# Expert-choice hybrid block: unread products of the router's results placed on TensorE between the steps of the choice of experts

## Chip, core and metric

The kernel runs on one core of a Trainium2 chip. The metric is device time in microseconds (us) of one execution. Engines are named as in the profile: PE is TensorE's matmul part, PEld its weight load, DVE is VectorE, ACT is ScalarE, POOL is GpSimd, SP is SyncE, whose queue (SPq) issues most DMAs.

## What is computed

Two layers of a hybrid backbone over 512 tokens of 1024 channels (256 context tokens, 256 latent tokens). After the token mixers, the output projection and a layer norm, each layer runs an expert-choice mixture of experts. The change stands inside the choice:

```
def expert_choice_ffn(u, w_router, w_e1, w_e3, w_e2):
    cap = EC_CAPACITY * n_tok // N_EXPERTS                 # 2 * 256 // 16 = 32
    aff = jax.nn.softmax((u @ w_router).astype(jnp.float32), axis=-1)
    gate, idx = lax.top_k(jnp.swapaxes(aff, 1, 2), cap)    # 32 tokens for each of 16 experts
    xs = u[bidx, idx]
    h = jax.nn.silu(einsum('becd,edf->becf', xs, w_e1)) * einsum('becd,edf->becf', xs, w_e3)
    y = einsum('becf,efd->becd', h, w_e2) * gate[..., None]
    return jnp.zeros_like(u).at[bidx, idx].add(y)
```

Layer 0 does this for the context and for the latent tokens, each with its own choice; layer 1 for the latent tokens alone, and only they are the output.

## The kernel before, in words

The layers run one after the other (`layer`). In each, attention, retention, HGRN2 and RWKV-7 are computed first, then the branches are merged, and the last third is the expert stage: `out_proj` (output projection, layer norm and, by `logits`, the router's products), `route` (the choice), `experts` (16 experts in a loop).

**The choice, `route`.** It is one chain. Router logits lie in `lg` with tokens on the 128 partitions; the softmax over 16 experts is five steps: the maximum `mx` (profile: tile `rmx`, L1516), the difference (L196, `tt`), the exponential on ACT (L193), the sum `sm` (tile `rsm`, L1519), its reciprocal **in place** (L1520) and the product. Two TensorE transposes turn the result so that experts lie on partitions; DVE copies it to `aft` (tile `pa`, L1529). Then four rounds find the 32 largest of 256 affinities per expert, eight a round:

```
m8 = T([64, 8], "m8", bufs=2)
for i in range(CAP // 8):
    src = aft if i == 0 else wk
    nc.vector.max(m8[R], src[R])
    nc.vector.match_replace(wk[R], m8[R], src[R], -1.0)
```

`m8` is taken from its pool once, ahead of the loop: all four rounds write the same tile (profile: tile `m`, L1535 the maximum, L1536 the replacement). Then come a comparison, a running sum (L1539) and a product that give each chosen token its slot, two transposes back (`w<-ident,pa`), a copy to `pt` (L1546), and the first `gather`: one-hot matrices `oh` from `pt`, and products `h<-oh,x` that collect the tokens of the first four experts into `xg`. `R` is rows 0 to 63 in layer 0 and 32 to 63 in layer 1.

**The experts.** Each of the 16 has three 1024x1024 fp32 weights, 12 units of 1 MB, which SP's queue fetches in order into a ring of rooms (`ring`, `mid`, `low`, `late`, in layer 1 also `pair`; `expert_weights`, L1600 and L1604). A unit's DMA is issued when its room's last reader has finished. The ring is filled ahead while `route` runs; after that a fetch waits for the products of an expert.

**PSUM.** In the expert stage three tags share it: `h` (3 banks), `y` (2), `w` (3). `self.mm` (L211) is one matmul; an fp32 matmul shows as two records in the trace. The order of each engine's queue is that of the program. A tile that is overwritten waits for its readers, on whatever engine they are.

Of the kernel before, what the change touches and what calls it, by code (L numbers as in the profile page):

```python
# [18 lines left out]
P = 128  # L19
# [157 lines left out]
class Block:  # L177
# [1321 lines left out]
    def route(self, l, lo, x, sc, sh, lg, xg, pool, xpool):  # L1499


        nc = self.nc
        t0, s0 = lo // 128, lo // 256
        r0 = 32 * s0
        ns = 2 - s0
        pa = pool.tile([64, 2, 256], F32, tag="pa", name="pa")
        pos, aft = pa[:, 0], pa[:, 1]
        T = lambda shape, tag, dt=F32, bufs=1: pool.tile(shape, dt, tag=tag, name=tag, bufs=bufs)
        lv = lg[:, t0:, :].rearrange("p (s j) e -> p s j e", j=2)
        tmp = xpool.tile([P, 1024], F32, tag="oht", name="tmp")  # L1510
        af = tmp[:, 0:128].rearrange("p (j s e) -> p j s e", j=2, s=2)
        mx, sm = T([P, ns, 2], "rmx"), T([P, ns, 2], "rsm")
        nc.gpsimd.memset(af, 0.0)

        av = af.rearrange("p j s e -> p s j e")[:, s0:, :, 0:E]
        nc.vector.tensor_reduce(mx, lv, AX.X, ALU.max)  # L1516
        self.tt(av, lv, mx.unsqueeze(3).to_broadcast([P, ns, 2, E]), ALU.subtract)
        self.act(av, av, AF.Exp)
        nc.vector.tensor_reduce(sm, av, AX.X, ALU.add)  # L1519
        nc.vector.reciprocal(sm, sm)  # L1520
        self.tt(av, av, sm.unsqueeze(3).to_broadcast([P, ns, 2, E]), ALU.mult)
        ps = self.psum("w")
        for j in range(2):
            self.tr(ps[0:64, 128 * j:128 * j + 128], af[:, j].rearrange("p s e -> p (s e)"))
        R = slice(r0, 64)
        if s0:
            nc.gpsimd.memset(aft[0:32], 0.0)
            nc.gpsimd.memset(pos[0:32], -1.0)
        nc.vector.tensor_copy(aft[R], ps[R, 0:256])  # L1529

        wk, mk, ones = [tmp[0:64, 256 * i:256 * i + 256] for i in (1, 2, 3)]
        m8 = T([64, 8], "m8", bufs=2)
        for i in range(CAP // 8):
            src = aft if i == 0 else wk
            nc.vector.max(m8[R], src[R])  # L1535
            nc.vector.match_replace(wk[R], m8[R], src[R], -1.0)  # L1536
        self.ts(mk[R], wk[R], 0.0, ALU.is_lt)
        nc.gpsimd.memset(ones, 1.0)
        nc.vector.tensor_tensor_scan(pos[R], ones[R], mk[R], 0.0, ALU.mult, ALU.add)  # L1539
        self.tt(pos[R], pos[R], mk[R], ALU.mult)  # L1540

        ps = self.psum("w")
        for j in range(2):
            self.tr(ps[:, 64 * j:64 * j + 64], pos[:, 128 * j:128 * j + 128])
        pt = T([P, 2, 2, 32], "pt")
        nc.vector.tensor_copy(pt.rearrange("p j s e -> p (j s e)"), ps[:, 0:128])  # L1546

        def gather(e0, dst, tag):

            n = dst.shape[2]  # L1550
            w = 32 * n
            whole = w < 256
            if not whole:
                room = xpool.tile([P, 2, 4, 256], F32R, tag="hl", name="xhl", bufs=1)
            for s in range(s0, 2):
                if not whole or s == s0:
                    ohs = xpool.tile([P, 1 + whole, 2, n, 32], F32 if whole else F32R, tag="oht", name="oh", bufs=1)
                oh = ohs[:, whole and s]
                for j in range(2):
                    self.tt(oh[:, j], pt[:, j, s, e0:e0 + n].unsqueeze(2).to_broadcast([P, n, 32]),  # L1560
                            self.iota.unsqueeze(1).to_broadcast([P, n, 32]), ALU.is_equal)
                for k in range(KT):
                    xk = x[:, 2 * s - t0:2 * s - t0 + 2, 128 * k:128 * k + 128]
                    xs = [xk]
                    if not whole:
                        xs = [room[:, i, k % 4].rearrange("p (t c) -> p t c", c=128) for i in range(2)]
                        self.split(*xs, xk)
                    ps = self.psum(tag)[:, 0:w]
                    for j in range(2):
                        for v in xs:  # L1570
                            self.mm(ps, v[:, j], oh[:, j].rearrange("p e c -> p (e c)"), start=(j == 0 and v is xs[0]),
                                    stop=(j == 1 and v is xs[-1]))
                    d = dst[:, k, :, 32 * (s - s0):32 * (s - s0) + 32]
                    src = ps.rearrange("p (e c) -> p e c", c=32)
                    if k % 2:
                        self.act(d, src, AF.Identity, bias=sh[:, k, s:s + 1], scale=sc[:, k, s:s + 1])
                    else:
                        self.ts(d, src, sc[:, k, s:s + 1], ALU.mult, sh[:, k, s:s + 1], ALU.add)

        gather(0, xg, "h")  # L1580
        return pa, gather
# [472 lines left out]
```

## Time and profile before

| | |
|---|---|
| time of 3 runs, median | 2281.23 us (2278.9 to 2287.31) |
| the profiled execution's own time | 2285.33 us |
| its span, first to last instruction | 2283.5 us |
| mean granted TensorE clock | 0.930 |
| busy: PE, DVE, ACT, POOL | 88%, 46%, 28%, 12% |
| DMA, mean over the span | 243 GB/s, 554.90 MB |

The span lies 1.8 us under the execution's own time. A granted clock of 1.00 is TensorE's higher level, 2.4 GHz, and 0.50 the lower, 1.2 GHz. Times in the rows are microseconds from the start of the span. Layer 0's choice lies at 792 to 812, layer 1's at 1826 to 1841.

### The profile page before, as it was taken

Reading aid. Unit: us, or ns where it says so; the run is one execution under the profiler, and the core shown is the slowest. Engines: PE = TensorE matmul, PEld = TensorE weight load, DVE = VectorE, ACT = ScalarE, POOL = GpSimd, SP = SyncE. Lnnn points to the kernel's source line nnn. Section 1 sums busy time; section 2 is a strip of 40 time slices with the busy share of each in tenths; the row PEclk is TensorE's granted clock in tenths of the full one; section 3 lists DMA queues with packets and bytes.
Section 4 is the critical chain, followed back from the end, with each engine's and each line's share of the span. In section 5 each row is a group of like instructions: output and inputs, shape, how many; then the busy total and the mean of one; then the engine's idle time right before and its main releaser. Section 6 shows DMA issues by size and latency. Waiting matters only on the chain. (4 is left out here: it accounts for less than half of the span.)

```text
span 2283.5 us, 38233 instructions
## 1 busy us (share of the span) xinstructions
PE 2004.9 (88%) x16294; PEld 1263.6 (55%) x16294; DVE 1039.2 (46%) x2174; ACT 630.4 (28%) x1044; POOL 270.8 (12%) x188
## 2 busy tenths in 40 slices
PE   6998999999999899999998898999899887676675
PEld 3657747777687744333332656777788753222222
DVE  3548755855523526222222666758764642020112
ACT  3453445413323212000000454464343320000000
POOL 2000201222242000000000200103353000000000
PEclk8999999999999999999999899998999889777777
DMA  8264242111252587999999555224223899999996
GB/s 321 84 218 149 80 129 79 36 48 60 103 191 88 230 350 304 426 425 425 426 426 424 203 171 191 67 76 151 87 92 130 319 389 423 425 424 424 424 424 280
DMA packets 96939, 554.90 MB, mean 243 GB/s; under 512 B 11296, under 2 KB 13280, under 8 KB 46848
## 3 DMA queue, kind: packets, MB, share of 16 engines
q1 hardware_dynamic: 95312, 543.93, 61.1%
q0 software_dynamic: 912, 6.42, 0.7%
q8 instruction: 128, 2.10, 0.4%
q10 hardware_dynamic: 544, 2.10, 0.3%
q14 instruction: 43, 0.35, 0.0%
HBM read 549.13 MB, written 3.28 MB: 242 GB/s over the span
## 5 line engine op out<-in xcount | busy, mean ns | idle before, releaser
L221 POOL TENSOR_TENSOR wl<-wr,wh 128x1280 fp32r<-128x1280 f32 (+1 forms) x62 | 179.1, 2888 | 317.0 <-ACT wh L193 314.0
L211 PE MATMUL m<-mh,wh 128*128 128x512 f32 (+1 forms) x512 | 190.0, 371 | 6.0 <-ACT th L193 5.0
L193 ACT ACTIVATE wh<-wr 128x1024 fp32r<-128x1024 f32 (+1 forms) x126 | 143.3, 1138 | 157.4 <-PE pj L211 69.4
L211 PE MATMUL m<-mh,wl 128*128 128x512 f32 (+1 forms) x512 | 177.6, 347 | 2.5 <-POOL wl L221 1.9
L211 PE MATMUL m<-ml,wh 128*128 128x512 f32 (+1 forms) x512 | 177.3, 346 | 0.0
L211 PE MATMUL h<-late,later 128*32 128x256 f32 (+1 forms) x880 | 139.5, 538 | 30.0 <-DMA late<-in_w_e_dram 29.8
L206 DVE SCALAR_TENSOR_TENSOR h<-h 128x512 f32<-128x512 f32 (+1 forms) x32 | 17.7, 554 | 299.8 <-ACT h L193 299.8
L221 DVE TENSOR_TENSOR wl<-wr,wh 128x1024 fp32r<-128x1024 f32 (+1 forms) x64 | 78.9, 1235 | 103.9 <-ACT wh L193 103.3
L193 ACT ACTIVATE h<-h 128x512 f32<-128x512 f32 (+1 forms) x32 | 15.7, 491 | 396.9 <-PE h L211 396.9
L211 PEld LDWEIGHTS m<-mh,wh 128*128 128x128 f32 x512 | 100.8, 197 | 32.4 <-issue 14.4
L196 DVE TENSOR_TENSOR h<-h 128x512 f32<-128x512 f32 (+1 forms) x32 | 17.7, 554 | 214.5 <-PE h L211 214.5
L211 PE MATMUL h<-ring,later 128*32 128x256 f32 (+1 forms) x640 | 94.0, 543 | 19.7 <-DMA ring<-in_w_e_dram 19.7
L211 PEld LDWEIGHTS m<-mh,wl 128*128 128x128 f32 x512 | 100.8, 197 | 13.2 <-POOL wl L221 2.1
L211 PEld LDWEIGHTS m<-ml,wh 128*128 128x128 f32 x512 | 101.1, 198 | 10.8 <-issue 2.3
L211 PEld LDWEIGHTS h<-late,later 128*32 128x32 f32 (+1 forms) x880 | 44.2, 134 | 113.3 <-issue 58.4
L193 ACT ACTIVATE ht<-w 128x512 f32<-128x512 f32 (+1 forms) x32 | 15.7, 491 | 281.7 <-PE w L216 281.7
L211 PE MATMUL y<-late,ht 128*32 128x256 f32 (+1 forms) x536 | 71.9, 494 | 8.4 <-DMA late<-in_w_e_dram 5.8
L211 PE MATMUL h<-mid,later 128*64 128x512 f32 (+1 forms) x352 | 64.2, 555 | 12.5 <-DMA mid<-in_w_e_dram 12.5
L211 PEld LDWEIGHTS h<-ring,later 128*32 128x32 f32 (+1 forms) x640 | 30.4, 137 | 73.3 <-issue 36.3
L211 PE MATMUL y<-ring,ht 128*32 128x256 f32 (+1 forms) x448 | 58.8, 492 | 13.1 <-DMA ring<-in_w_e_dram 9.7
L193 ACT ACTIVATE th<-m 128x512 f32<-128x512 f32 (+1 forms) x50 | 24.7, 493 | 164.8 <-PE m L211 164.5
L206 DVE SCALAR_TENSOR_TENSOR ht<-y,gt,g 128x512 f32<-128x512 f32 (+1 forms) x32 | 18.7, 614 | 95.9 <-PE y L211 95.7
(636 smaller groups left out, 4508.2 us busy)
## 6 DMA issues: line engine op xcount, KB each, us to landing
late<-in_w_e_dram SPq DMA_DIRECT2D x144, 1024.0 KB, 19.5
ring<-in_w_e_dram SPq DMA_DIRECT2D x109, 1024.0 KB, 19.7
mid<-in_w_e_dram SPq DMA_DIRECT2D x63, 1024.0 KB, 19.7
pair<-in_w_e_dram SPq DMA_DIRECT2D x36, 1024.0 KB, 19.6
wr<-in_wmg_dram SPq DMA_DIRECT2D x48, 640.0 KB, 4.0
mw<-in_wmod_dram SPq DMA_DIRECT2D x48, 512.0 KB, 5.8
y<-in_wmod_dram SPq DMA_DIRECT2D x48, 512.0 KB, 4.3
low<-in_w_e_dram SPq DMA_DIRECT2D x20, 1024.0 KB, 19.8
```

Of the source, the lines that this page charges most:

```text
L193: self.nc.scalar.activation(out=out, in_=in_, func=func, **kw)
L196: self.nc.vector.tensor_tensor(out, a, b, op)
L206: self.nc.vector.scalar_tensor_tensor(out, a, s, b, op0, op1)
L211: self.nc.tensor.matmul(out, lhsT, rhs, start=start, stop=stop)
L221: (eng or self.nc.vector).tensor_tensor(lo, src, hi.bitcast(F32), ALU.subtract)
```

## The change

A helper `warm(v)` in `route` issues three matmuls of 256 columns each. Their weights (the stationary operand) are a result of the chain, `v`; what streams through are rows of `x`, the block of normalised tokens. The sums go to a PSUM tile of tag `y` that nothing reads. It is called after `mx`, after `sm`, and in each of the four rounds after the maximum: six times a layer, 18 matmuls, in both layers.

```
+        def warm(v):
+            ps = self.psum("y")
+            v = v.rearrange("p a b -> p (a b)") if len(v.shape) == 3 else v
+            R = slice(r0, 64) if v.shape[0] < P else slice(0, P)
+            for i in range(3):
+                self.mm(ps[0:v.shape[1], 0:256], v, x[R, 0, 256 * (i % 2):256 * (i % 2) + 256])
...
         nc.vector.tensor_reduce(mx, lv, AX.X, ALU.max)
+        warm(mx)
         self.tt(av, lv, mx.unsqueeze(3).to_broadcast([P, ns, 2, E]), ALU.subtract)
         self.act(av, av, AF.Exp)
         nc.vector.tensor_reduce(sm, av, AX.X, ALU.add)
+        warm(sm)
         nc.vector.reciprocal(sm, sm)
...
             nc.vector.max(m8[R], src[R])
+            warm(m8[R])
             nc.vector.match_replace(wk[R], m8[R], src[R], -1.0)
```

On PE, in layer 0's `route` (layer 1's is the same with 2 columns of `rmx` and `rsm`); `wrt,u` are the router's products, `tmp` the softmax, `m` the eight maxima, `pa` the slots:

```order
 L211 MATMUL h<-wrt,u 128x16 x3
+L211 MATMUL y<-x_5595,rmx 4x256 [waits DVE_49]
+L211 MATMUL y<-x_5595,rmx 4x256 x2
+L211 MATMUL y<-x_5595,rsm 4x256 [waits DVE_49]
+L211 MATMUL y<-x_5595,rsm 4x256 x2
 L216 MATMUL w<-ident,tmp 64x128 [waits DVE_49,Pool_49]
 L216 MATMUL w<-ident,tmp 64x128
-L216 MATMUL w<-ident,pa 128x64 [waits DVE_49,PE_49]
+L211 MATMUL y<-x_5595,m_6885 8x256 [waits DVE_49,PE_49]
+L211 MATMUL y<-x_5595,m_6885 8x256 x2
+L211 MATMUL y<-x_5595,m_6885 8x256 [waits DVE_49]
+L211 MATMUL y<-x_5595,m_6885 8x256 x2
```

Six matmuls stand ahead of the first pair of transposes, and twelve (two of the four rounds are shown) between that pair and the next.

On DVE, at the same place, from the sum of the softmax to the second round:

```order
-L1520 RECIPROCAL rsm<-rsm 128x4 [waits DVE_49]
+L1529 TENSOR_REDUCE rsm<-tmp 128x4 [waits Activation_49]
+L1531 RECIPROCAL rsm<-rsm 128x4 [waits DVE_49,PE_49]
 L196 TENSOR_TENSOR tmp<-tmp,rsm 128x2x2x16 [waits DVE_49]
...
+L1546 MAX m_6885<-pa 64x8 [waits DVE_49]
+L1548 MATCH_REPLACE tmp<-m_6885,pa 64x256 [waits DVE_49]
+L1546 MAX m_6885<-tmp 64x8 [waits DVE_49,PE_49]
+L1548 MATCH_REPLACE tmp<-m_6885,tmp 64x256 [waits DVE_49]
```

No DVE instruction is added or moved, but four of them now also wait for PE in each layer: the reciprocal, which overwrites the weights `rsm`, and the maxima of rounds two, three and four, which overwrite the weights `m`. The queues of ACT, POOL and SP stand as before.

## Rows read from the trace of the kernel before

**Rows 1.** The page's 40 slices of the span, granted TensorE clock in tenths:
```profile
PEclk8999999999999999999999899998999889777777
```
**Rows 2.** Windows over layer 0's choice: busy of engines, granted clock, DMA share, GB/s:
```profile
core 0: us, PE busy (x) PEld busy (x) DVE busy (x) ACT busy (x) POOL busy (x), PEclk, DMA share, GB/s
790.00:792.00 2.00, 1.28 (x8) 1.28 (x8) 1.57 (x6) 1.17 (x2) 0.00 (x0) 0.81 0.97 406
792.00:794.00 2.00, 0.16 (x1) 0.05 (x1) 1.31 (x7) 1.46 (x4) 0.46 (x2) 0.50 1.05 442
794.00:800.00 6.00, 0.60 (x2) 0.18 (x2) 4.80 (x16) 0.00 (x0) 0.00 (x0) 0.50 1.00 421
808.00:812.00 4.00, 4.00 (x37) 4.00 (x36) 1.64 (x4) 1.87 (x5) 0.00 (x0) 0.96 0.13 53
```
**Rows 3.** Windows over layer 1's choice, same columns:
```profile
1826.00:1828.00 2.00, 0.11 (x1) 0.00 (x0) 1.20 (x7) 1.52 (x4) 0.48 (x2) 0.50 0.99 418
1838.00:1842.00 4.00, 4.00 (x41) 3.62 (x44) 1.84 (x5) 1.83 (x4) 0.00 (x0) 0.86 0.53 223
```
**Rows 4.** Timeline of DVE in layer 0's choice: start, us, engine, line, operation:
```profile
792.47 0.22 DVE L1516 TENSOR_REDUCE rmx<-lg 128x4 f32<-128x64 f32 x1
793.76 0.18 DVE L1520 RECIPROCAL rsm<-rsm 128x4 f32<-128x4 f32 x1
795.44 0.42 DVE L1535 MAX8 m<-pa 64x8 f32<-64x256 f32 x1
796.40 0.42 DVE L1535 MAX8 m<-tmp 64x8 f32<-64x256 f32 x1
798.34 0.42 DVE L1535 MAX8 m<-tmp 64x8 f32<-64x256 f32 x1
800.41 0.42 DVE L196 TENSOR_TENSOR pa<-pa,tmp 64x256 f32<-64x256 f32 x1
```
**Rows 5.** Timeline of PE, PEld and first readers in layer 0's choice and gather:
```profile
794.31 0.18 PEld L216 LDWEIGHTS w<-ident,tmp 128*64 128x64 f32 x2 [2.26 <-issue]
800.94 0.28 PEld L216 LDWEIGHTS w<-ident,pa 64*128 64x128 f32 x2 [6.45 <-issue]
802.12 10.35 PE L211 MATMUL h<-oh,x 128*128 128x128 f32 x64 [0.71 <-DVE oh L196]
803.38 0.41 DVE L202 TENSOR_SCALAR xg<-h,ra,rb 128x128 f32<-128x128 f32 x1 [0.71 <-PE h L211]
806.79 0.41 DVE L202 TENSOR_SCALAR xg<-h,ra,rb 128x128 f32<-128x128 f32 x1 [1.30 <-PE h L211]
```
**Rows 6.** Timeline of layer 1's gather, first expert products and their reader:
```profile
1836.08 5.28 PE L211 MATMUL h<-oh,x 128*128 128x128 f32 x32 [0.71 <-DVE oh L196]
1841.29 3.66 PE L211 MATMUL h<-pair,xg 128*32 128x256 f32 x64
1844.76 2.77 PE L211 MATMUL h<-ring,xg 128*32 128x256 f32 x48
1845.01 0.39 ACT L193 ACTIVATE h<-h 128x256 f32<-128x256 f32 x1 [3.16 <-PE h L211]
```
**Rows 7.** SP's queue after layer 0's choice, and layer 1's issue (timeline):
```profile
794.11 22.31 SPq L1604 DMA_DIRECT2D ring<-in_w_e_dram  x3
1843.28 2.55 SPq L1604 DMA_DIRECT2D pair<-in_w_e_dram  x4
```
**Rows 8.** Windows of both expert stages, columns as in rows 2:
```profile
808.50:814.40 5.90, 5.90 (x46) 4.55 (x46) 3.06 (x7) 2.29 (x5) 0.00 (x0) 1.00 0.01 4
812.00:910.00 98.00, 97.23 (x479) 41.89 (x479) 41.02 (x83) 15.93 (x34) 0.00 (x0) 1.00 0.83 326
910.00:1240.00 330.00, 310.41 (x1400) 105.97 (x1397) 82.73 (x156) 22.50 (x37) 0.12 (x1) 1.00 1.01 425
1844.00:2266.00 422.00, 302.06 (x3328) 127.06 (x3324) 62.05 (x152) 24.98 (x60) 0.00 (x0) 0.80 1.00 419
1999.50:2009.80 10.30, 7.86 (x72) 2.61 (x68) 0.42 (x1) 0.39 (x1) 0.00 (x0) 0.50 1.02 422
```

## The prediction

> **What bounds the kernel now.** I read the page first, then windows over the two choices of experts, then the timeline of each choice, last what follows it. The page's clock slices [rows 1] stand at 9 or 10 tenths nearly everywhere, and low in the last quarter; nothing there shows the choice, which is some 20 us of 2283. The windows do [rows 2, 3]: from 792 to 800 and from 1826 on the granted clock is 0.50, the lower of TensorE's levels (1.2 GHz), and PE is nearly idle while DVE runs the chain. In layer 0 the clock had fallen just before, inside 790 to 792 (mean 0.81), so the stretch begins cold whatever is put into it. The gather after the chain then starts cold. By the mean of 0.96 in 808 to 812 layer 0's clock rose at 808.3 (4 us x 0.04 / 0.5 = 0.3 us cold), 6.2 us after the gather began at 802.12 [rows 2, 5]; layer 1's rose at 1839.1 (0.86, so 1.1 us cold), 3.0 us after 1836.08 [rows 3, 6].
>
> The choice is on the path that sets the end, in both layers. In layer 1 the first fetch that waits for expert 0's products is issued at 1843.28, and from 1844 to 2266 the DMA share is 1.00 [rows 7, 8]: whatever delays that issue delays the end by as much. In layer 0 the queue's three `ring` fetches begin at 794.11 and take 22.31 us to be issued, since they wait for rooms, and from 808.5 to 814.4 the DMA engines move 4 GB/s [rows 7, 8]: the fetches made ahead have landed, so none covers a later gather. Then PE is busy 97.2 of 98 us up to 910 at clock 1.00, and after that DMA runs at 1.01 [rows 8]. Both start from the gather's end. So I count each microsecond of the chain once, in either layer, and half a percent (11.4 us, about what a measurement of this kernel can tell from no change) is a lot of chain.
>
> **Prices.** A new batch is three fp32 matmuls of 256 columns, six records. No row before has weights of 4 or 8 columns, so I go by columns streamed. Cold, sixteen records of 128 columns lie between the readers at 803.38 and 806.79: 0.213 us each, so 0.426 for 256 columns and **2.56 us a batch** [rows 5]. At the upper level (2.4 GHz) 64 records of 256 columns, four side by side, start over 3.47 us, 0.217 a step, so **1.30 us a batch** [rows 6]. Those are the two ends; that narrow weights make it cheaper I exclude, since a record's length follows what streams, and all six use the same columns and can't stand side by side. A PE instruction follows its DVE source by 0.11 us (`pa` ends at 800.83, its load starts at 800.94) [rows 4, 5]. A reader follows the end of the stream by 0.41 us cold (802.12 + 4 x 0.213 = 802.97, reader at 803.38) and by 0.25 warm (1844.76 to 1845.01) [rows 5, 6].
>
> **The change part by part.** It removes nothing. It adds six batches a layer, and waits of DVE for PE that the order shows at four places.
>
> *The reciprocal* overwrites `rsm`, the second batch's weights, so it waits for that batch, which queues behind the first. `rmx` ends at 792.69, the reciprocal now starts at 793.76, 1.07 later [rows 4]. Cold: 0.11 + 2 x 2.56 + 0.41 = 5.64, so 4.6 us later. If the clock rises 3.0 us into the batches, as in layer 1's gather, 7 records go cold and 5 warm: 0.11 + 3.0 + 1.08 + 0.25 = 4.44, 3.4 later. If it rises after 6.2 us, as in layer 0's gather, that is too late to help. I take the middle, **+4.0**. Behind the reciprocal on DVE stands only the chain itself; ACT and POOL have nothing else to do there, and SP waits for rooms.
>
> *The rounds.* `m8` is one tile, so the next maximum waits until the last matmul of the batch before is done. A round is 0.96 us now (795.44 to 796.40) [rows 4]. With the batch in it: 0.42 (the maximum) + 0.11 + 2.56 + 0.41 = 3.50 cold, +2.54; or 0.42 + 0.11 + 1.30 + 0.25 = 2.08 warm, +1.12. The replacement, 0.48, hides beside the batch. Three maxima wait: **+7.6** cold, +3.4 warm. Which? Between the softmax batches and the first round lie two transposes, a copy and a maximum, some 2 us with PE nearly idle, and in such an idle stretch the clock fell in both layers. Once cold, a round keeps PE at work for 2.56 of 3.50 us, 73%; the nearest row is 1999.5 to 2009.8, busy 7.86 of 10.3 us, 76%, and the clock stayed at 0.50 through it [rows 8]. So I take cold.
>
> A gap of its own between groups of matmuls is what the Trainium skill ("TensorE: Matmul & The Clock Gate", section "A second HAM failure mode: psum-queue depth-cycling") describes: it says that frequent short idling between groups makes the clock swing between its levels. By it the rounds would cost the mean, 3 x 1.83 = 5.5 instead of 7.6, and the sum below would be 18.4 instead of 22.6; the row just named speaks for the lower level.
>
> *The fourth batch* has no maximum behind it, but the transposes of `pa` stand behind it on PE. They start 2.18 us after the fourth maximum ends (798.76 to 800.94) [rows 4, 5]; the batch needs 0.11 + 2.56 = 2.67: **+0.5** cold, nothing warm, where DVE's comparison, scan and product cover it.
>
> *The gather* is what could gain. All warm it would be 64 x 0.108 = 6.9 us instead of 10.35 in layer 0, and 32 x 0.108 = 3.5 instead of 5.28 in layer 1 [rows 5, 6]: 5.2 us in all, the most there is to win. With cold rounds it starts cold again, after PE has been at work, so I take layer 1's 3.0 us before the rise for both: layer 0 saves 3.2 us of half rate, **-1.6**, layer 1 nothing.
>
> PSUM, ACT, POOL and SP cost nothing: the `y` banks are not read until expert 0's third product.
>
> **Sum.** 4.0 + 7.6 + 0.5 = 12.1 a layer, 24.2 for both, less 1.6: **+22.6 us**. The profiled execution took 2285.3 us, so 2307.9 on its own terms; it stands 4.1 above the median of the three runs, so 2303.8 against the median, 1.0% slower.
>
> **Rivals.**
>
> *The clock holds.* It rises in the softmax batches (+3.4), stays up in the rounds (+3.4, where a warm round keeps PE at work 1.30 of 2.08 us) and through the gather (-5.2 in all): 2 x 6.8 - 5.2 = +8.4, 2289.6. For it: the gathers show that products do raise the clock. Against: the 2 us of idle PE in between. The Trainium skill, same page, section "Why this matters for your kernels", advises to leave no idle gap between bursts so that the clock stays up; that is the rule for this rival, and the trace agrees with its first half: with PE idle the clock stood at 0.50 [rows 2, 3]. Even so the waits cost more than the gather returns.
>
> *One layer holds, the other not.* 6.8 - 3.4 + 12.1 in one case, 10.5 + 6.8 - 1.8 in the other: +15.5 both, 2296.7.
>
> *Products with 4 or 8 columns of weights don't raise the clock at all.* No row has such weights alone. Then 4.6 + 7.6 + 0.5 = 12.7 a layer, and layer 1's gather may run cold to its end (32 x 0.213 = 6.8, +1.5): +26.9, 2308.1.
>
> *The other side: the wait ends with the weight load.* If DVE were let go once the last of a batch's weights are in the array, the rounds would keep their 0.96 us and PE would run behind. At the upper level throughout, the first transposes would start 0.11 + 2.60 = 2.71 us after `rmx` instead of 1.62, +1.1, and four batches (5.2 us) would end 0.2 us late for `pa`: +1.3 a layer, -5.2 by the gathers, so -2.6, 2278.6. It decides where a release comes under 0.5 us after the maximum, as the replacement takes that long. Against it: an array that still streams uses its weights, and the order names PE as a whole. That the delay vanishes behind fetches (no change, the change then not doing anything) is of the same size; the DMA gap [rows 8] speaks against it.
>
> **How the numbers follow.** Forecast (cold rounds, 22.6) 0.54; nothing raises the clock 0.15; one layer holds 0.13; the clock holds in both 0.11; the other side and no effect 0.07. Slower by over 0.5%: the first three, and 0.02 of the fourth, where runs scatter: 0.84. Within: 0.09 + 0.05 = 0.14. Faster: 0.02. The range runs from the clock holding in both, 2290, to nothing raising it, 2308, and a microsecond for scatter: 2290 to 2309.
>
> **What would show it.** Right: the reciprocal 4 to 5.7 us after `rmx`, maxima 3.5 us apart, clock 0.50 over most of the rounds, the gather starting 12 us later in each choice than `rmx` now implies, DMA idle longer before the first fetch of the expert stage, and the stretch after it as long as before. Wrong: maxima 1 us apart (no wait), or 2.1 us apart at clock 1.00 with gathers of 7 and 3.5 us (the clock holds), or a delay that the later stretches don't pass on.

## The result and the profile after

The changed kernel takes **2301.32 us** (median of 6 runs, 2298.22 to 2306.87), the kernel before 2280.07 (6 runs, 2278.33 to 2287.31): a ratio of **1.0084, interval 1.0067 to 1.0101**, so 19.2 us more (15.3 to 23.0). The forecast was 22.6 more, 2303.8.

DVE's timeline over layer 0's choice (against [rows 4]) shows where the time went (layer 0, then layer 1):

```profile
787.78 0.22 DVE L1525 TENSOR_REDUCE rmx<-lg 128x4 f32<-128x64 f32 x1
792.31 0.18 DVE L1531 RECIPROCAL rsm<-rsm 128x4 f32<-128x4 f32 x1 [3.21 <-PE y L211]
793.76 0.42 DVE L1546 MAX8 m<-pa 64x8 f32<-64x256 f32 x1
795.81 0.42 DVE L1546 MAX8 m<-tmp 64x8 f32<-64x256 f32 x1 [1.12 <-PE y L211]
797.78 0.42 DVE L1546 MAX8 m<-tmp 64x8 f32<-64x256 f32 x1 [1.04 <-PE y L211]
801.02 0.42 DVE L1546 MAX8 m<-tmp 64x8 f32<-64x256 f32 x1 [2.30 <-PE y L211]
...
1833.09 0.19 DVE L1525 TENSOR_REDUCE rmx<-lg 128x2 f32<-128x32 f32 x1
1838.65 0.17 DVE L1531 RECIPROCAL rsm<-rsm 128x2 f32<-128x2 f32 x1 [4.30 <-PE y L211]
1840.06 0.42 DVE L1546 MAX8 m<-pa 32x8 f32<-32x256 f32 x1
1842.11 0.42 DVE L1546 MAX8 m<-tmp 32x8 f32<-32x256 f32 x1 [1.12 <-PE y L211]
1845.34 0.42 DVE L1546 MAX8 m<-tmp 32x8 f32<-32x256 f32 x1 [2.31 <-PE y L211]
1848.58 0.42 DVE L1546 MAX8 m<-tmp 32x8 f32<-32x256 f32 x1 [2.31 <-PE y L211]
```

The four waits stand where the order said, each released by PE's `y<-x` products. The reciprocal starts 4.31 us after `rmx` ends (788.00), before 1.07. The maxima are 2.05, 1.97 and 3.24 us apart, before 0.96; in layer 1 they are 2.05, 3.23 and 3.24. The sizes 2.0 and 3.2 are the two levels of the clock, as PE's timeline shows (against [rows 5, 6]):

```profile
788.05 2.72 PE L211 MATMUL y<-x,rmx 128*4 128x256 f32 x6 [0.90 <-DVE rmx L1525]
790.57 1.70 PE L211 MATMUL y<-x,rsm 128*4 128x256 f32 x6
796.29 1.46 PE L211 MATMUL y<-x,m 64*8 64x256 f32 x6 [0.51 <-DVE m L1546]
798.26 2.72 PE L211 MATMUL y<-x,m 64*8 64x256 f32 x6 [0.51 <-DVE m L1546]
804.15 0.48 PE L216 MATMUL w<-ident,pa 64*128 64x64 f32 x2
805.33 10.35 PE L211 MATMUL h<-oh,x 128*128 128x128 f32 x64 [0.71 <-DVE oh L196]
815.62 2.80 PE L211 MATMUL h<-ring,xg 128*64 128x512 f32 x12
...
1852.89 5.31 PE L211 MATMUL h<-oh,x 128*128 128x128 f32 x32 [0.71 <-DVE oh L196]
1858.13 3.66 PE L211 MATMUL h<-pair,xg 128*32 128x256 f32 x64
```

A batch takes 2.72 us in the records at the lower level and 1.46 at the upper. The gathers are what they were: 10.35 and 5.31 us. The windows (columns as in [rows 2]) give the clock:

```profile
788.00:790.00 2.00, 1.95 (x5) 0.60 (x6) 0.45 (x2) 0.85 (x2) 0.00 (x0) 0.50 0.98 414
790.00:792.00 2.00, 2.00 (x8) 0.64 (x6) 0.00 (x0) 0.00 (x0) 0.00 (x0) 0.74 1.04 438
796.00:798.00 2.00, 1.46 (x6) 0.44 (x6) 0.93 (x4) 0.00 (x0) 0.00 (x0) 0.97 1.03 434
798.00:800.00 2.00, 1.74 (x5) 0.57 (x6) 0.68 (x3) 0.00 (x0) 0.00 (x0) 0.50 0.99 418
804.00:806.00 2.00, 1.29 (x6) 0.96 (x6) 1.19 (x5) 0.00 (x0) 0.00 (x0) 0.50 0.01 4
810.00:812.00 2.00, 2.00 (x13) 2.00 (x13) 0.70 (x2) 0.46 (x1) 0.00 (x0) 0.62 0.00 0
```

The softmax batches do raise it: 0.74 over 790 to 792 puts the rise at 791.0, 3.0 us after the first product. It then holds over the idle stretch and two rounds, falls at 797.9, and rises again only inside the gather. In layer 1 it rises at 1838.9, 0.3 us after the softmax batches have ended, and falls after one round. The DMA share is 0.01 from 804 on: the fetches made ahead have landed, as in [rows 8], and the delay goes through to SP's queue (against [rows 7]):

```profile
1860.12 2.60 SPq L1616 DMA_DIRECT2D pair<-in_w_e_dram  x4
```

Call "the choice" the time from the end of `rmx` to expert 0's first product. It took 27.62 and 24.85 us here, 19.71 and 14.61 in the profile of before (792.69 to 812.40 and, by [rows 6], 1826.68 to 1841.29): 18.1 us more of the 19.2. Expert 0's first product in layer 0 before:

```profile
812.40 3.65 PE L211 MATMUL h<-ring,xg 128*64 128x512 f32 x16
```

What follows the second choice lasts as long as ever (442.17 us, before 442.21).

### The profile page after: what moved, and what is told of

Read it like the earlier page. It is cut to its first block, busy times and chain, and to the rows that moved or that the text cites. A ratio compares the mean times of both kernels' runs of the same rounds, so it can differ in the third digit from the quotient of the medians.

```text
span 2300.3 us, 38385 instructions
## 1 busy us (share of the span) xinstructions
PE 2029.4 (88%) x16366; PEld 1268.8 (55%) x16366; DVE 1037.0 (45%) x2174; ACT 629.9 (27%) x1044; POOL 271.3 (12%) x188
## 6 DMA issues: line engine op xcount, KB each, us to landing
mid<-in_w_e_dram SPq DMA_DIRECT2D x63, 1024.0 KB, 19.7
low<-in_w_e_dram SPq DMA_DIRECT2D x20, 1024.0 KB, 19.8
```

## Experiments

Diffs are against the changed kernel unless said otherwise.

**The parts alone.** `e2_softmax_only` keeps the two softmax batches, `e3_rounds_only` the four in the rounds, `e4_one_product` all six, each of one product:

```
 e2:  -            warm(m8[R])
 e3:  -        warm(mx)      -        warm(sm)
 e4:  -            for i in range(3):      +            for i in range(1):
```

> The batches in the four rounds are left out, the two in the softmax stay. Theory: the reciprocal starts 4.4 to 5.1 us after rmx ends, instead of 1.1, the maxima stand 0.96 us apart, the clock falls again before the gather, which takes its 10.4 and 5.3 us or up to 2 us more or less: +3.3 and +4.0, together about +7 us (5 to 10). Rival, the loss sits in the rounds alone: 0 to +2 us.

> The two batches in the softmax are left out, those in the four rounds stay. Theory: the softmax is as before, the first round starts at the lower clock and nothing in the rounds raises it, as TensorE works 2.6 of 3.4 us: maxima 3.2 to 3.5 us apart in all three waits of both layers, transposes of pa 0.5 us late, +7.4 to +8.1 a layer, together about +15.5 us (13 to 17). If instead the batches raise the clock by themselves, maxima of 2.0 us appear in the later rounds and the sum lies near +9.

> One product in a batch instead of three. Theory (the price goes by the columns streamed, in the wait of DVE): reciprocal 2.2 us after rmx ends (+1.1), maxima 1.7 to 1.8 us apart (+0.8 each, three times), pa's transposes not late: +3.6 a layer, about +7 us in both (5 to 9). Rival, the price is that of a wait between the engines and not of the products: maxima as far apart as in the changed kernel (2.0 to 3.2 us) and +12 us or more. Rival, TensorE's queue alone: the transposes half a microsecond late, +1 us in all.

Measured: ratios of 1.005 (1.0028 to 1.0072), 1.0066 (1.0043 to 1.0089) and 1.0035 (1.0019 to 1.0052). In e2 the reciprocal starts 4.54 and 5.37 us after `rmx`, the maxima are 0.97 apart and the choices 22.31 and 20.03 us. In e3 every round is cold, 3.24 us, and the choices are 27.01 and 22.25. Its window shows the clock through such rounds:

```profile
790.00:796.00 6.00, 4.53 (x12) 1.11 (x12) 2.21 (x7) 0.00 (x0) 0.00 (x0) 0.50 1.01 422
```

What follows: each part costs by itself, and both by the same wait. PE is busy 4.53 of 6 us in e3's rounds and its clock stays at 0.50. In the changed kernel the first rounds were warm because the softmax batches had raised it. In e4 rounds of 1.53 to 1.62 us show that a wait remains even for two records. Against the mean of two profiles of before (the table below) the choices cost 8.3, 15.3 and 6.0 us, each inside its expected range; the time of e2, 11.4 us more, lies above its range of 5 to 10, with an interval of 6.4 to 16.4.

**The wait taken away.** `e1_own_tiles` gives each batch weights that nobody overwrites, so DVE never waits:

```
-        nc.vector.reciprocal(sm, sm)
+        rs = T([P, ns, 2], "smr")
+        nc.vector.reciprocal(rs, sm)
...
         for i in range(CAP // 8):
+            m8 = T([64, 8], f"m8{i}")
```

> Each round writes maxima of its own tile, and the reciprocal writes a tile of its own, so no DVE step waits for a batch; the 36 products stay where they are. Theory (DVE waits for the batches whose weights it would overwrite): the reciprocal starts 1.1 us after rmx ends, the maxima stand 0.96 us apart in both layers, the transposes still queue behind the two softmax batches (about +3 us a layer), the four later batches run on without gaps beside DVE (0 to +5 us) and the gathers start at the upper clock (-3.4 and -1.8 us). Sum over both layers about +2 us on the kernel before (0 to +8), so some 15 us less than the changed kernel. Rival, TensorE's own queue delays the chain: as the changed kernel, +15 to +21. Rival, the streams slow DVE's steps by contention: the maximum takes clearly over 0.42 us and most of the loss stays.

Measured: 1.0078 (1.0055 to 1.0102), nearly the whole loss. The waits are gone (reciprocal +1.11, maxima 0.96 to 0.97 apart), but the choices still take 26.61 and 21.49 us. PE's timeline and windows of layer 0:

```profile
798.41 8.41 PE L211 MATMUL y<-x,m 64*8 64x256 f32 x24 [1.06 <-DVE m L1547]
806.75 0.47 PE L216 MATMUL w<-ident,pa 64*128 64x64 f32 x2
...
798.00:800.00 2.00, 1.59 (x8) 0.71 (x9) 1.86 (x7) 0.00 (x0) 0.00 (x0) 1.00 1.00 422
800.00:801.00 1.00, 1.00 (x5) 0.31 (x4) 0.93 (x4) 0.00 (x0) 0.00 (x0) 0.74 1.02 426
801.00:807.00 6.00, 6.00 (x16) 1.80 (x14) 2.04 (x6) 0.00 (x0) 0.00 (x0) 0.50 1.01 423
810.00:814.00 4.00, 4.00 (x21) 4.00 (x20) 0.82 (x2) 1.37 (x3) 0.00 (x0) 0.50 0.00 0
```

PE's own queue took the place of the wait: the transposes of `pa` stand behind 24 records that run 8.41 us, and start 5.58 us after the last maximum instead of 2.21. The surprise is the clock. It fell at 800.5 with PE busy without a gap, and stayed at 0.50 for six more microseconds of unbroken products. So the theory had the waits right and its sum (about 2 us) wrong: the gathers, which it had at the upper level, began cold, and the batches held up the transposes of `pa` by 3.3 to 3.4 us in each layer. The time is that of the rival in which TensorE's own queue delays the chain; but part of it lies outside the choices, as the table below shows.

**How many rows the products use.** The batches of the rounds take 64 of the 128 rows of TensorE in layer 0 and 32 in layer 1; the softmax batches take all. `e6_128_rows` makes the rounds' products 128 rows high, the added rows of weights zero, and keeps the waits; `e5_own_128` does the same with the tiles of e1:

```
 e6:  +        m8 = T([P, 8], "m8", bufs=2)
      +        nc.gpsimd.memset(m8, 0.0)
      -            warm(m8[R])
      +            warm(m8)
```

> The changed kernel with weights of all 128 rows in the rounds, one tile as before, so the maxima still wait. New theory: the clock stays at 1.00 through the rounds, maxima 2.0 us apart in all three waits of both layers, the gathers at about 7 and 3.5 us: +3 in layer 0 and +5.5 in layer 1, about +8.5 us (6 to 12), which is the rival of the prediction in which the clock holds. Rival (rows don't matter): as the changed kernel, rounds of 3.2 us and +18.

> Own tiles as in the first experiment, and in the four rounds the weights span all 128 rows (8 maxima on their rows, zeros on the others), so each batch streams 128 rows of x instead of 64 or 32; columns, places and count are the same. New theory (products over 64 or 32 rows neither raise nor hold the clock, those over 128 rows do): clock 1.00 from the end of the softmax batches on, the four batches take 1.30 us each and end about with pa (2.2 to 2.6 us after the last maximum instead of 5.5), the gathers take about 7 and 3.5 us: +0 to +2.5 a layer by the softmax batches alone, +2.5 us in all (0 to +8), against the +13.8 that the two choices took longer with own tiles alone. Rival (narrow weights don't hold the clock, whatever their rows): clock 0.50 under the batches, as with own tiles alone, +13 or more.

Measured: e6 1.0041 (1.0025 to 1.0057), e5 1.003 (1.0013 to 1.0047). DVE's maxima of e6 in layer 0, then e5's PE timeline and windows there:

```profile
795.58 0.42 DVE L1547 MAX8 m<-pa 64x8 f32<-64x256 f32 x1
797.64 0.42 DVE L1547 MAX8 m<-tmp 64x8 f32<-64x256 f32 x1 [1.13 <-PE y L211]
799.61 0.42 DVE L1547 MAX8 m<-tmp 64x8 f32<-64x256 f32 x1 [1.04 <-PE y L211]
801.59 0.42 DVE L1547 MAX8 m<-tmp 64x8 f32<-64x256 f32 x1 [1.04 <-PE y L211]
```

```profile
792.64 5.34 PE L211 MATMUL y<-x,m 128*8 128x256 f32 x24 [1.05 <-DVE m L1550]
798.96 7.41 PE L211 MATMUL h<-oh,x 128*128 128x128 f32 x64 [0.71 <-DVE oh L196]
...
792.00:794.00 2.00, 1.36 (x7) 0.63 (x8) 1.84 (x7) 0.00 (x0) 0.00 (x0) 1.00 0.99 418
794.00:798.00 4.00, 4.00 (x20) 1.56 (x19) 3.18 (x9) 0.00 (x0) 0.00 (x0) 1.00 1.02 426
798.00:800.00 2.00, 1.29 (x11) 1.15 (x12) 1.48 (x6) 0.00 (x0) 0.00 (x0) 1.00 1.03 430
```

The same 24 records take 5.34 us instead of 8.41, with no fall of the clock, and the gather is warm from its first product: 7.41 us instead of 10.35 (layer 1: 3.81 to expert 0's first product, where the changed kernel has 5.24). All four choices of e5 and e6 hold 1.00 from the rounds to the gather's end. e6's choices are 23.24 and 19.31 us, e5's 19.92 and 16.00.

**Fills without a chain.** Would products that wait for nothing gain? `g1_fill` drops `warm` and puts two products at the output projection's last tile, five before the first transposes, twelve after them, all over 128 rows; `g2_fill64` has the twelve over 64 rows (`fill(n, v)` issues n products of 256 columns with the weights `v`; nothing reads them):

```
+            if t == 3:
+                ps = self.psum("h")
+                for i in range(2):
+                    self.mm(ps[0:8, 0:256], self.ident[:, 0:8], x[:, 256 * i:256 * i + 256])
...
+        fill(5, self.ident[:, 0:8])
...
+        fill(12, tmp[:, 0:8])
```

> No weights that a step overwrites: products of 256 columns over 128 rows, with constant weights between the router's last products and ahead of the first transposes, and twelve with the softmax's result as weights between the two pairs of transposes; none has a DVE step behind it. Theory: the clock stays at 1.00 from the output projection to the gather, the chain is as long as before (at most 0.5 us longer), the gathers take about 7 and 3.5 us: 5 us less than before (-2 to -6), 0.2%. If the clock falls in the softmax all the same: twelve products at the lower clock take 10 us where there are 6, and +4 to +8.

> As the fill before, but the twelve products between the transposes run over 64 rows instead of 128 (weights and x). Nothing else differs. Theory (rows count): the clock falls within the twelve products, they end after pa is ready (0 to 3 us late), and the gathers start cold again, 9 to 10.4 and 5 to 6 us: 0 to +6 us against before, and 4 us or more over the fill with 128 rows. Rival: the same as the fill with 128 rows.

Measured: 1.0011 (0.9995 to 1.0027) and 1.0006 (0.999 to 1.0022), neither told from no change; the 5 us that g1 was to gain did not come. In g1's layer 0 the clock is 1.00 throughout and the choice takes 16.31 us, 3.4 less than before. In layer 1 it takes 15.26, as windows of g1 there show:

```profile
1826.00:1828.00 2.00, 1.20 (x6) 0.32 (x4) 1.76 (x8) 0.00 (x0) 0.00 (x0) 1.00 1.01 426
1828.00:1830.00 2.00, 0.31 (x2) 0.20 (x2) 1.44 (x4) 0.00 (x0) 0.00 (x0) 0.99 1.01 426
1830.00:1832.00 2.00, 1.67 (x8) 1.70 (x9) 0.79 (x3) 0.00 (x0) 0.00 (x0) 0.50 1.03 434
```

The products ran ahead of the chain (six records of the twelve products, written behind the first transposes, ran before them), held up those transposes by 0.9 us (2.55 after `rmx`), and ended at 1827.2; PE was nearly idle from there on, and at 1830.0 the clock fell, just ahead of the gather. g2's twelve were to lose the clock while they ran, and did not, in either layer: it stayed at 1.00 through 5.3 us of them in layer 0 and fell in the gather, at 806.2; in layer 1 it stayed at 1.00 through 5.8 us of them (with the first transposes in between) and fell at 1840.4, in the idle stretch behind them (choices 17.95 and 16.44 us). So its theory failed: products over 64 rows don't bring a fall every time. In g2 PE had been at work over 128 rows ahead of the twelve, with the clock at 1.00; in e1 and its repeat the clock had been up for only 1.0 to 2.5 us when the batches of the rounds began. No run tells whether that is the difference.

`g3_hold` combines the two: g1's first fills (but three before layer 1's transposes), and in the rounds 3, 3, 3 and 2 products over 128 rows with weights in four tiles of their own:

```
+        ms = [T([P, 8], f"m8{i}") for i in range(CAP // 8)]
...
+            src, m8 = aft if i == 0 else wk, ms[i]
...
+            fill(3 - (i == 3), m8)
```

> Products that hold the clock without a wait of DVE: fills over all 128 rows, with the identity's columns as weights where no result of the chain is needed (two at the output projection's last tile, five in layer 0 and three in layer 1 ahead of the first transposes), and in the rounds three, three, three and two products whose weights are four tiles of their own, 128 rows high, so that each batch starts after its maximum and no maximum waits. Theory (row count and the gaps of PE set the clock; waits of DVE and the queue of PE set the loss): maxima 0.96 us apart, reciprocal 1.1 us after rmx, first transposes at most 0.3 us late, those of pa at most 0.3 late, granted clock 1.00 from the output projection to the end of both gathers, gathers 7.3 and 3.8 us instead of 10.3 and 5.2; the choices together 3 to 5 us shorter than before, the time 0.1 to 0.2% under before. Rival (the fills cost on PE what the gathers return, as in the fill kernel's layer 1): choices within 1 us of before, ratio 1.000. Second rival (the clock falls in the gaps between the small batches): 0.50 within the rounds, gathers of 9 us and more in layer 0, and the choices longer than before.

Measured: 1.0012 (0.9998 to 1.0027), no gain. Layer 0 went as the theory has it (choice 16.18 us, gather 7.34). In layer 1 the clock fell at 1829.4 (0.85 over 1828 to 1830), in the idle stretch before the rounds. The 22 records took 7.79 us, so that the transposes of `pa` started 4.89 us after the last maximum instead of 2.21. But these products, over 128 rows, raised the clock again at 1836.2, 5.9 us after the first of them, and the gather was warm (3.81 us); the choice took 15.26. Together the choices are still 2.9 under the first profile of before, and the time does not show it.

**What scatters.** Three kernels were profiled a second time.

> The kernel before once more, for a second profile of the stretches outside the choices. Theory (what the kernels differ by outside their choices is scatter of single executions): the choices last 19.7 and 14.6 us again within 0.3, while the start of layer 0's choice, the stretch between the choices and the one after the second differ from the first profile by 2 to 6 us. Rival (these stretches are fixed and the changed kernels lengthen them): they repeat within 1 us.

> The changed kernel once more. Theory (the clock's rise and fall in the choice are set by what PE did before, not by chance): reciprocal 4.3 and 5.4 us after rmx, maxima 2.0, 2.0, 3.2 us apart in layer 0 and 2.0, 3.2, 3.2 in layer 1, gathers 10.3 and 5.2 us, choices 27.6 and 24.9 us long, all within 0.3. Rival (the moment of the fall scatters): the number of rounds that run at the upper level differs from the first profile, by 1.2 us of choice for each; the choices then lie between 23 us and 29 us.

> The kernel with a weight tile of its own for every batch once more, since the moments of the clock's rise and fall turned out to scatter from one execution to the next. Theory (products over 64 or 32 rows don't raise the clock): after the fall, granted clock 0.50 to the end of the batches although PE is busy without a break for more than 4 us, in both layers; last maximum to the transposes of pa 4.5 to 5.9 us; gathers over 8.8 and over 4.9 us; the choices at least 24 and 20 us long. Rival (the first profile's low clock was chance): in at least one layer the clock rises within the batches, those transposes come 2.5 us after the last maximum as with 128 rows, and that gather takes 7.3 or 3.8 us.

`s1_before_again`: `rmx` of layer 0 ends at 804.32, before 792.69, so what precedes the choice scatters by 11.6 us. The choices take 18.34 and 15.33 us (before 19.71 and 14.61). They did not repeat within 0.3: the clock's rise in the gather moved, by 1.4 us of choice in layer 0 and 0.7 the other way in layer 1, while the sum moved by 0.7. `s2_after_again`: 29.69 and 25.46 us, so the rival was right that the number of warm rounds is not fixed, though 29.69 lies above its 29. Its maxima in layer 0:

```profile
796.56 0.42 DVE L1546 MAX8 m<-pa 64x8 f32<-64x256 f32 x1
798.94 0.42 DVE L1546 MAX8 m<-tmp 64x8 f32<-64x256 f32 x1 [1.45 <-PE y L211]
802.18 0.42 DVE L1546 MAX8 m<-tmp 64x8 f32<-64x256 f32 x1 [2.30 <-PE y L211]
805.41 0.42 DVE L1546 MAX8 m<-tmp 64x8 f32<-64x256 f32 x1 [2.31 <-PE y L211]
```

Only part of the first round is warm here. `s3_own_again`, which is e1 once more: 25.12 and 18.70 us. In layer 0 as in e1; in layer 1 the clock held over 4.4 us of products over 32 rows and then fell, again with PE busy:

```profile
1836.70:1839.00 2.30, 2.27 (x11) 0.96 (x12) 2.16 (x7) 0.00 (x0) 0.00 (x0) 1.00 1.01 427
1839.00:1841.00 2.00, 2.00 (x11) 0.77 (x9) 1.79 (x6) 0.00 (x0) 0.00 (x0) 1.00 1.01 422
1841.00:1842.00 1.00, 1.00 (x4) 0.35 (x3) 0.50 (x2) 0.00 (x0) 0.00 (x0) 0.55 0.98 410
1842.00:1843.00 1.00, 1.00 (x5) 0.19 (x2) 0.00 (x0) 0.00 (x0) 0.00 (x0) 0.50 1.06 442
```

There the theory's lower bounds (4.5 us to the transposes, choices of 24 and 20) were missed: 3.34 us, and 18.70 in layer 1. What repeats in all four choices with own tiles over 64 or 32 rows is the fall under unbroken work, and a cold start of the gather (8.96 to 10.28 us, 5.18 to 5.63).

**A loss that is not in the choice.** Set side by side, over both layers and against the mean of the two profiles of before (34.0 us), the time against its median of 2280 us:

| kernel | choices, us more | time, us more (interval) | fetch rate, GB/s, 960 to 1240 us |
|---|---|---|---|
| changed (2 profiles) | +19.8 | +19.2 (15.3 to 23.0) | 426 |
| e1 (2 profiles) | +12.0 | +17.8 (12.5 to 23.3) | 421 |
| e2 | +8.3 | +11.4 (6.4 to 16.4) | 425 |
| e3 | +15.3 | +15.0 (9.8 to 20.3) | 426 |
| e4 | +6.0 | +8.0 (4.3 to 11.9) | 426 |
| e5 | +1.9 | +6.8 (3.0 to 10.7) | 421 |
| e6 | +8.6 | +9.3 (5.7 to 13.0) | 425 |
| g1 | -2.4 | +2.5 (-1.1 to 6.2) | 425 |
| g2 | +0.4 | +1.4 (-2.3 to 5.0) | 425 |
| g3 | -2.6 | +2.7 (-0.5 to 6.2) | 421 |

The kernels with four tiles of their own lose 5 to 6 us more than their choices do. All four profiles of them fetch the experts' weights at 421 GB/s, all ten others at 425 or 426. The page's rate slices and the row of its issues, the changed kernel's and then e1's:

```profile
GB/s 319 89 213 146 92 115 78 48 47 60 165 133 135 231 299 311 426 425 425 426 425 408 172 185 184 69 113 116 81 98 152 325 313 424 425 424 423 424 424 282
late<-in_w_e_dram SPq DMA_DIRECT2D x144, 1024.0 KB, 19.5
```

```profile
GB/s 319 95 211 142 83 124 78 48 47 48 146 157 121 237 299 306 422 421 421 421 421 420 197 175 194 57 110 120 86 96 146 327 337 420 421 421 421 421 421 289
late<-in_w_e_dram SPq DMA_DIRECT2D x144, 1024.0 KB, 19.8
```

The bytes are the same; a unit lands 0.3 us later. 1.0% of the 330 us of layer 0 that DMA bounds [rows 8] is 3.3 us, and the stretch after the second choice is 443.8 to 444.5 us in those four profiles, 440.8 to 442.2 in the others: 2.6 more. Sum 5.9. (g1's difference is as large at 425, within its interval of 3.7 either way: it is the rate that shows the loss, not the differences.) In the built programs the small tiles move one kind of room, `late`, which takes 144 of the 384 units: its rooms start at a multiple of 256 bytes of a partition in before, the changed kernel, e2, e3, e4, e6, g1 and g2, 96 bytes behind one in e1 and e5, 64 in g3. All other rooms stay, 64 or 128 bytes off. The Trainium skill ("DMA: Bandwidth & Descriptors", section "How a descriptor splits into AXI transactions") says that a descriptor which does not start at a multiple of 256 bytes spends beats on bytes that it fetches and throws away. It does not say whether that holds for the side that is written, and only that side moved here. By its way of counting, a row of 8 KB that starts 96 bytes off takes 259 beats instead of 256, which over 144 of 384 units is an estimate of 0.4%, less than half of what the rates show. No run moved the rooms alone, so the cause is argued and not shown.

## Why the prediction was right

The sign, the place and the size held, the size in part by luck: the rounds were 2.0 us a layer too dear, and the 1.6 us that the gather was to give back did not come, which made up for some of it. By its steps, with the two profiles of the changed kernel against the first of before:

- *The waits.* Four a layer, as forecast; the rival on the other side, that DVE is let go with the weight load, is out: maxima 2 to 3.2 us apart. Without those waits (e1) the choices are 7.8 us shorter, over 128 rows (e6 to e5) 6.6.
- *The reciprocal*, +4.0: measured +3.2, +4.3, +4.1 and +3.4, mean 3.75. The bounds of 3.4 and 4.6 held but for 0.2, and the clock rose 3.0 to 5.6 us after their first product, in three choices inside these batches and once 0.3 us behind them.
- *The rounds*, +7.6: **the mis-sized term**. Measured +4.4, +5.6, +6.0 and +6.5, mean 5.6. A cold round is 3.24 us, not 3.50: it is 0.42 for the maximum, 0.05 until PE starts, 2.72 of records and 0.04 until DVE goes on, where I had put 0.41 after the stream. That makes 0.8 of the 2.0. The rest is the step "in such an idle stretch the clock fell", by which all rounds were to begin cold: the clock, raised by the softmax batches, outlasted the idle stretch and fell inside the rounds, after two, one and twice only part of a warm one. The rows that this step went by show the clock falling ahead of the idle stretch, with PE still busy for 1.28 of 2 us [rows 2]. The step behind it, "Once cold", held: no cold round was followed by a warm one, and in e3 all of them are cold. The rule of the Trainium skill ("TensorE: Matmul & The Clock Gate", section "A second HAM failure mode: psum-queue depth-cycling") that the clock swings where groups of matmuls are short of work in between gave 5.5, the better number, by luck. The trace agrees with it only in part: the clock falls once and does not come back in the rounds, and with the same gaps over 128 rows (e6) it does not fall.
- *The fourth batch*, +0.5: 2.71 us to the transposes of `pa` instead of 2.21, in all four choices.
- *The gather*, -1.6: it did not come. 10.29 and 5.24 us, again 9.93 and 5.88; before 10.28 and 5.21, again 8.84 and 5.92. That PE was at work ahead of it did not hasten the rise.

The sum of the measured terms is 2 x (3.75 + 5.6 + 0.5) = 19.7, against 19.8 of the choices and 19.2 of the time. The rival "the clock holds" (+8.4) is what e6 built: +8.6 in the choices, +9.3 in the time. The rival that 4 columns of weights do not raise the clock is out: products with 2 and 4 columns over 128 rows raised it in all four choices of the changed kernel.

What the prediction did not see is why the clock did not hold. It put the cold rounds down to the gaps, PE at work 73% of a round. With the same gaps and 128 rows (e6) it held, and without gaps at 64 and 32 rows (e1) it fell. The two causes add up, in microseconds of both choices over before:

| | 64 and 32 rows | 128 rows |
|---|---|---|
| DVE waits | +19.8 (changed) | +8.6 (e6) |
| no wait | +12.0 (e1) | +1.9 (e5) |

The rows are worth 10 to 11 us, the waits 7 to 8. That is rough: each kernel with 128 rows was profiled once, and the two profiles of e1 differ by 4.3 us in their choices.

## What to carry to other kernels

Filler work that reads a result of the chain makes whoever next overwrites that result wait for the whole product; and even without that wait it stands in its engine's queue ahead of the chain's own next step, so price both. Before filler is put in to hold a clock, look whether the filler as shaped holds it (here products over part of the rows lost it in all eight choices of the changed kernel and e1, and kept it while they ran in both of g2), and what the most is that can be won: about 4 us of 2283 here, by the warm gathers of e5 and e6 (7.34 and 3.81 us, where the two profiles of before have 10.28 and 8.84, and 5.21 and 5.92); the prediction had worked out 5.2. After any edit that adds a tile, compare the fetch rate, too: a loss there shows in no step of the change.

## What was not expected of the hardware

- TensorE's clock fell to 0.50 while PE was busy without a gap, in all four choices with unbroken batches over 64 or 32 rows (e1 and its repeat), and in three of the four it stayed there for 5.7 to 6.3 us of further products. With 128 rows, most of the weights zero, it was 1.00 in all four choices of e5 and e6, and in g3's layer 1 such products raised it again. In both layers of g2 it held over 5.3 us and more of 64-row products, so what sets the moment of the fall stays open.
- Zero rows of weights cost nothing seen: at the upper level six records took 1.45 or 1.46 us over 32, 64 and 128 rows alike.
- The rise comes at no fixed time: in 8 gathers of before, the changed kernel and their repeats it came 2.8 to 5.9 us after the first product, worked out as twice what the gather took over 7.34 us in layer 0 and over 3.81 in layer 1.
- A shift of 64 or 96 bytes in where `late` rooms start went with 421 GB/s of fetches instead of 425.

Open: a version that beats the kernel before was not found. g3 with its `late` rooms where they were might be one (choices 2.6 us shorter), but that is about 0.1%, less than its 12 runs told apart (0.15% either way), and it was not tried.
